# Where the row scale and the first two SwiGLU gates are issued in the opening of each FFN

## The chip, the cores and the metric

The kernel runs on one core of one Trainium2 chip. The time is the device time of one execution of the whole program in microseconds (us); each number for a kernel is the median of several runs. The core has five engines that each work off a queue of their own in order: TensorE (PE in the profile; PEld is its loading of weights), VectorE (DVE), ScalarE (ACT), GpSimd (POOL) and SyncE (SP), which here only issues transfers. They wait for each other through semaphores. SBUF is the on-chip memory; PSUM is the accumulator memory, eight banks of 128 x 512 floats.

## What is computed

A decoder trunk of two layers over 512 tokens of width 1024. Each layer is a half-step SwiGLU FFN, a token mixer (retention in layer 0, forgetting attention in layer 1), a second half-step FFN and a gated per-layer input (PLE). So there are four FFNs, FFN 0 to FFN 3. What matters here is one of them:

```
def rmsnorm(x, w):
    y = x * lax.rsqrt(jnp.mean(x * x, axis=-1, keepdims=True) + EPS)
    return y * w

def swiglu(x, w_in, w_out):
    g, u = jnp.split(x @ w_in, 2, axis=-1)
    return (jax.nn.silu(g) * u) @ w_out

h = h + 0.5 * swiglu(rmsnorm(h, nw[0]), ffn_w_in[i, 0], ffn_w_out[i, 0])
```

The inner width is 2816, which makes 22 pairs of 128 gate rows and 128 up rows.

## The kernel before

Everything is kept transposed, features on the partitions and the 512 tokens along the free axis. Each float32 operand is split into a high and a low part (`split`, line 299: ACT writes the rounded high part, L302; DVE the difference, L303), and a product is made of three matmuls. Weights come through `wraw` tiles (SP's queue, L75), are split by ACT and DVE (L82, L83) or by ACT and an accumulating transfer that GpSimd issues (L120 to L122), and stand in a pool of three tiles, two ahead of use.

The norm's gain is applied to the input, but its scale, one number for each token, is applied after the matmuls. It is made in two steps. `Norm.columns` (line 441) sums the squares on PE (L326) and takes the reciprocal root on ACT and DVE (L464 to L468), which gives `cols`, the scale with tokens on partitions. `Norm.rows` (line 450) transposes `cols` on PE, four matmuls of 128 x 128 into a bank (L459), and ACT copies them to `rows` (L453), in which form the gates use it.

An FFN (`ffn`, line 503) goes through its 22 pairs. The first two are plain (`plain`, line 511): 96 matmuls of 256 columns for one pair (L524), over 16 steps (k, t) of six matmuls. The other 20 pairs use Strassen's form in Winograd's variant with seven products instead of eight, twelve matmuls of 256 columns each (`product`, L493). It is cut into `one` (two products), `two` (one product, and then part of the recombination: ACT copies g to `cc`, L542; DVE adds it to u, L543; ACT copies the sum, L545; DVE adds that to g, L546), `three` (four products into the same banks g and u) and `finish` (the rest of the recombination and the gate). The sums of weights that these products need are made on DVE (L151) and split like the rest (`emit_sums_now`, line 142); in FFN 0 DVE and ACT also make the input's Strassen forms (`quarters`, line 369: L376, L377 and the lines around them) while the plain pairs run.

`gated` (line 564) is the SwiGLU gate of one pair: DVE multiplies g by `rows` (L566), ACT takes the Silu (L567, which loads its table when another function's was in use), DVE multiplies by u (L569 or L571), and `split` makes the two parts (L302, L303) that the output blocks multiply later.

The opening of an FFN stands at lines 592 to 602. In order of issue: the first plain pair, `columns`, the second plain pair, `rows`, `one` of the first Strassen pair (pair 2), the gates of both plain pairs (0 and 1), `two` of pair 2. Then the loop of line 604 issues `one` and `two` of pair 3, `three` and `finish` of pair 2, and so on, one pair ahead; after six, fourteen and all 22 pairs come the output blocks (`out_blocks`).

Only PE's order is written by hand (`manual_schedule`, line 190). The order of ACT, DVE, GpSimd and SP is made when the program is built, by a planner that goes by the order of issue and by its own estimates of when an operand or a buffer is ready; on the chip each queue is then worked off in that order, and an instruction that waits holds what is behind it. Buffers come from pools: eight banks, seven tiles `tmp`.

Of the kernel before, what the change touches and what calls it, by code (L numbers as in the profile page):

```python
# [187 lines left out]
def trunk(ctx, tc, a):  # L188
# [18 lines left out]
    def unit(pool):  # L207
        return pool.tile([P, S], F32R, name="unit_" + {id(ua): "a", id(ub): "b", id(uc): "c", id(ud): "d"}[id(pool)])
# [78 lines left out]
    def bank():  # L287
        return psum.tile([P, S], F32, name="bank")

    def temp(dtype=F32):  # L290
        return tmp.tile([P, S], dtype, name="tmp")
# [7 lines left out]
    def split(src, hi, lo, scale=None):  # L299

        if scale is None:
            high = nc.scalar.copy(hi, src)  # L302
            low = nc.vector.tensor_tensor(out=lo, in0=src, in1=hi.bitcast(F32), op=ALU.subtract)  # L303
        else:
            high = nc.scalar.activation(hi, src, AF.Identity, scale=scale)
            low = nc.vector.scalar_tensor_tensor(
                out=lo, in0=src, scalar=scale, in1=hi.bitcast(F32), op0=ALU.mult, op1=ALU.subtract
            )
        return high, low

    def mm3(out, wh, wl, xh, xl, first, last):
        nc.tensor.matmul(out, wh, xh, start=first, stop=False)  # L312
        nc.tensor.matmul(out, wh, xl, start=False, stop=False)  # L313
        nc.tensor.matmul(out, wl, xh, start=False, stop=last)  # L314
# [175 lines left out]
    def product(out, w, c, forms, name, first=False):  # L490

        xs = [form[name] for form in forms]
        add = lambda w, x, start, stop: nc.tensor.matmul(  # L493
            out, w, x, start=start, stop=stop, skip_group_check=True
        )
        for j, (xh, xl) in enumerate(xs):
            wh = w[:, 0, c + j * P : c + (j + 1) * P]
            add(wh, xh, first and j == 0, False)
            add(wh, xl, False, False)
        for j, (xh, xl) in enumerate(xs):  # L500
            add(w[:, 1, c + j * P : c + (j + 1) * P], xh, False, j == 3)

    def ffn(i, n, nxt, stack, apool, meanwhile=None):


        ins, outs = ffn_src[i]
        chunks = CHUNKS[i]
        c0, c1 = HALVES
        live, act = {}, {}

        def plain(m):

            ws = [W.take(ins[m].q), W.take(ins[m].r)]
            g, u = bank(), bank()
            order = [(k, t) for k in range(KB) for t in range(2)]
            if i:
                order.sort(key=lambda kt: kt[1])
            for k, t in order:
                e = k % 2
                for o, (w, c) in ((g, (ws[e], 0)), (u, (ws[1 - e], 512))):  # L520
                    ks = slice(c + k // 2 * P, c + (k // 2 + 1) * P)
                    xh, xl = n.forms[k // 2][f"b{1 + e}{1 + t}"]
                    for q, (x, y) in enumerate(((w[0], xh), (w[0], xl), (w[1], xh))):
                        nc.tensor.matmul(  # L524
                            o[:, HALVES[t]], x[:, ks], y, start=k == t == q == 0, stop=k == KB - 1 and q == 2,
                            skip_group_check=True,
                        )
            return g, u

        def start(m):  # L530
            live[m] = W.take_pair(ins[m]), bank(), bank()

        def one(m):
            pair, g, u = live[m]
            product(g[:, c0], pair.t, 0, n.forms, "b11", True)
            product(g[:, c1], pair.s[0], 0, n.forms, "t1")

        def two(m):
            pair, g, u = live[m]
            product(u[:, c1], pair.s[1], 0, n.forms, "t2", True)  # L540
            cc = temp()
            nc.scalar.copy(cc, g)  # L542
            nc.vector.tensor_tensor(out=u[:, c1], in0=u[:, c1], in1=cc[:, c0], op=ALU.add)  # L543
            u2 = temp()[:, c0]
            nc.scalar.copy(u2, u[:, c1])  # L545
            nc.vector.tensor_tensor(out=g[:, c1], in0=g[:, c1], in1=u2, op=ALU.add)  # L546
            live[m] += (cc,)

        def three(m):
            pair, g, u, cc = live[m]  # L550
            product(u[:, c0], pair.t, 512, n.forms, "t4")
            product(g[:, c1], pair.s[3], 0, n.forms, "b22")
            product(u[:, c1], pair.s[2], 0, n.forms, "t3")
            product(g[:, c0], pair.x, 0, n.forms, "b21")

        def finish(m):
            pair, g, u, cc = live.pop(m)
            u3 = temp()[:, c0]
            nc.scalar.copy(u3, u[:, c1])
            nc.vector.tensor_tensor(out=u[:, c1], in0=u[:, c1], in1=cc[:, c1], op=ALU.add)  # L560
            nc.vector.tensor_tensor(out=u[:, c0], in0=u[:, c0], in1=u3, op=ALU.add)
            gated(m, g, u, False)

        def gated(m, g, u, change_sign):
            sg = temp()
            nc.vector.tensor_tensor(out=sg, in0=g, in1=n.r, op=ALU.mult)  # L566
            nc.scalar.activation(sg, sg, AF.Silu)  # L567
            if change_sign:
                nc.vector.scalar_tensor_tensor(out=sg, in0=u, scalar=-1.0, in1=sg, op0=ALU.mult, op1=ALU.mult)  # L569
            else:  # L570
                nc.vector.tensor_tensor(out=sg, in0=u, in1=sg, op=ALU.mult)  # L571
            hi, lo = unit(apool), unit(apool)
            split(sg, hi, lo)
            act[m] = hi, lo

        def out_blocks(c, ms):
            k0, k1 = chunks[c]
            os, ws = [bank() for _ in ms], [W.take(outs[c][m]) for m in ms]
            for k in range(k0, k1):
                js = slice((k - k0) * P, (k - k0 + 1) * P)  # L580
                for o, (wh, wl) in zip(os, ws):
                    mm3(o, wh[:, js], wl[:, js], *act[k], k == k0, k == k1 - 1)
            for m, o in zip(ms, os):
                t1 = temp()
                nc.vector.scalar_tensor_tensor(  # L585
                    out=t1, in0=o, scalar=-0.5, in1=n.r, op0=ALU.mult, op1=ALU.mult
                )
                nc.vector.tensor_tensor(out=h[m], in0=h[m], in1=t1, op=ALU.add)
                if c == len(chunks) - 1:
                    nxt.block(m)  # L590

        done = PLAIN[i]
        whole = [plain(m) for m in range(done - 1)]
        W.begin(n.columns())
        whole.append(plain(done - 1))
        n.rows()
        start(done)
        one(done)
        for m, (g, u) in enumerate(whole):
            gated(m, g, u, True)  # L600
        two(done)
        begun = done + 1
        for c, (k0, k1) in enumerate(chunks):
            for m in range(done, k1):
                if begun < k1:
                    start(begun)
                    one(begun)
                    two(begun)
                    begun += 1
                three(m)  # L610
                finish(m)
            done = k1
            if begun < NF:
                start(begun)
                one(begun)
                two(begun)
                begun += 1
            else:
                stack.close()
                if meanwhile:  # L620
                    meanwhile()
            for ms in ((0, 1), (2,), (3,), (4,), (5,), (6,), (7,)):
                out_blocks(c, ms)
# [588 lines left out]
    def ffn_ple(i, l, n, mid, nxt, stack, apool, parts):  # L1212
        phi, plo = [], []

        def load():
            pv = a["pT"][l].rearrange("(b p) t -> b p t", p=P)
            for b in range(2):
                t1 = temp()
                nc.sync.dma_start(out=t1, in_=pv[b])
                phi.append(unit(uc))  # L1220
                plo.append(unit(uc))
                split(t1, phi[b], plo[b])

        ffn(i, n, mid, stack, apool, load)
        stack = open_ffn(i + 1) if i < 3 else None
        ple(l, mid, nxt, phi, plo, parts)
        return stack

    ffn(0, norms[0], norms[1], stack, ud)
    stack = retention(norms[1], norms[2])  # L1230
    stack = ffn_ple(1, 0, norms[2], norms[3], norms[4], stack, ud, 1)
    ffn(2, norms[4], norms[5], stack, ua)
    stack = forgetting(norms[5], norms[6])
    ffn_ple(3, 1, norms[6], norms[7], norms[8], stack, ua, 2)
# [94 lines left out]
```

## Time and profile before

| | |
|---|---|
| median of 3 runs | 2216.24 us (2215.52 to 2218.65) |
| the profiled execution, its own time | 2215.98 us |
| its span, first to last instruction | 2214.2 us |
| mean granted clock of TensorE | 0.990 |
| PE idle in the span | 2214.2 - 2148.7 = 65.5 us |

The profile is one execution. A line of an engine's order of time gives the start from the span's begin, the time to the end of the group, engine, source line, operation, what it writes and reads, and how many instructions were merged; behind them in brackets is the idle time of the engine just before and who ended it. Instructions of one engine overlap a little, so that the distance from start to start is the pace. A line of the waits gives the engine and what it was to do, for whom it waited, and the total, the number and the longest of these waits.

### The profile page before, as it was taken

The page shows a single profiled execution, that of the slowest core. Times are in us where ns is not written, and L with a number is a line of the kernel's source. Part 1 is how long each engine was busy: PE and PEld are TensorE (multiplying, and loading weights), DVE is VectorE, ACT ScalarE, POOL GpSimd, SP SyncE. Part 2 cuts the span into 40 slices and gives each one's busy share as a digit, 9 for nine tenths or more (in the row PEclk, how much of TensorE's full clock was granted, in tenths as well). Part 3 has the DMA queues.
Part 4 walks back from the last instruction along what each step waited for, and adds up shares of the span by engine and source line. Part 5 has one row for each costly group of instructions (what it writes and reads, how often), then busy time and mean ns, then how long its engine had stood idle before and what let it go on. Part 6 is the DMA issues. An engine that isn't in the chain of part 4 may idle for free.

```text
span 2214.2 us, 34442 instructions
## 1 busy us (share of the span) xinstructions
PE 2148.7 (97%) x13525; PEld 1933.3 (87%) x13525; DVE 1459.4 (66%) x2631; ACT 1203.1 (54%) x2027; POOL 466.8 (21%) x352
## 2 busy tenths in 40 slices
PE   7999999999999999999998999999999999999997
PEld 7999997888888798989887989898788898999987
DVE  8687776352533677867758677675575686777764
ACT  7565453343333564746545646364786775554643
POOL 0011013444344000101142001012243200110154
PEclk9999999999999999999999999999999999999999
DMA  5465562222222244645523456373622234655631
GB/s 174 111 168 150 141 163 95 74 94 81 94 78 86 77 126 128 167 126 149 144 92 97 117 142 178 117 166 102 154 86 86 77 112 113 162 155 142 156 105 39
DMA packets 85315, 267.08 MB, mean 121 GB/s; under 512 B 9360, under 2 KB 12944, under 8 KB 85152
## 3 DMA queue, kind: packets, MB, share of 16 engines
q1 hardware_dynamic: 63328, 209.78, 28.0%
q0 software_dynamic: 20592, 54.01, 14.4%
q8 instruction: 106, 1.74, 0.3%
q10 hardware_dynamic: 1232, 1.09, 0.1%
q14 instruction: 57, 0.47, 0.1%
HBM read 262.71 MB, written 2.13 MB: 120 GB/s over the span
## 4 chain that ended last, share of the span: by engine, by line
PE 81%; DVE 7%; ACT 5%; issue 4%; DMA 3%; POOL 1%; SPq 0%; DVEq 0%; ACTq 0%; POOLq 0%
PE bank L493 31%; PE bank L314 13%; PE bank L312 13%; PE bank L313 13%; PE bank L524 3%; DMA wraw<-in_ffn_w_in 2%; PE bank L678 2%; PE bank L679 2%; PE bank L680 2%; DVE w L83 1%; POOL w L83 1%; ACT p L982 1%; ACT w L82 1%; DVE sums L151 1%; DVE tlo L303 1%
## 5 line engine op out<-in xcount | busy, mean ns | idle before, releaser
L82 ACT CAST w<-wraw 128x1024 fp32r<-128x1024 f32 (+1 forms) x242 | 245.5, 1022 | 439.7 <-PE bank L314 257.3
L314 PE MATMUL bank<-unit_a,w 128*128 128x512 f32 x736 | 287.9, 391 | 4.3 <-DVE w L83 2.6
L312 PE MATMUL bank<-unit_a,w 128*128 128x512 f32 x736 | 289.2, 393 | 1.9 <-ACT w L82 1.6
L313 PE MATMUL bank<-unit_a,w 128*128 128x512 f32 x736 | 287.2, 390 | 0.2 <-DVE unit_a L303 0.2
L83 POOL TENSOR_TENSOR w<-wraw,w 128x1024 fp32r<-128x1024 f32 x93 | 226.5, 2439 | 273.7 <-ACT w L82 259.6
L314 PE MATMUL bank<-unit_d,w 128*128 128x512 f32 (+1 forms) x712 | 267.8, 376 | 4.7 <-DVE w L83 4.7
L312 PE MATMUL bank<-unit_d,w 128*128 128x512 f32 (+1 forms) x712 | 268.9, 378 | 3.3 <-ACT w L82 1.6
L82 ACT CAST s<-sums 128x512 fp32r<-128x512 f32 x320 | 191.1, 617 | 146.6 <-DVE sums L151 100.8
L313 PE MATMUL bank<-unit_d,w 128*128 128x512 f32 (+1 forms) x712 | 268.0, 376 | 1.7 <-DVE unit_d L303 1.7
L83 DVE TENSOR_TENSOR s<-sums,s 128x512 fp32r<-128x512 f32 x320 | 213.8, 686 | 83.1 <-ACT s L82 82.0
L122 POOL DMA_DIRECT2D a<-in_ffn_w_in x80 | 70.3, 878 | 654.4 <-ACT a L121 448.0
L83 DVE TENSOR_TENSOR w<-wraw,w 128x1024 fp32r<-128x1024 f32 (+1 forms) x149 | 175.8, 1185 | 23.4 <-ACT w L82 23.3
L493 PE MATMUL bank<-unit_b,s 128*128 128x256 f32 x880 | 185.4, 277 | 0.0
L493 PE MATMUL bank<-unit_d,s 128*128 128x256 f32 x1140 | 178.3, 276 | 0.0
L493 PE MATMUL bank<-unit_a,s 128*128 128x256 f32 x1260 | 176.1, 277 | 1.9 <-ACT unit_a L376 1.1
L585 DVE SCALAR_TENSOR_TENSOR tmp<-bank,rows 128x512 f32<-128x512 f32 x96 | 66.1, 690 | 166.3 <-PE bank L314 165.1
L314 PEld LDWEIGHTS bank<-unit_a,w 128*128 128x128 f32 x736 | 138.5, 188 | 35.7 <-DVE w L83 4.4
L312 PEld LDWEIGHTS bank<-unit_a,w 128*128 128x128 f32 x736 | 138.6, 188 | 32.3 <-ACT w L82 3.5
L313 PEld LDWEIGHTS bank<-unit_a,w 128*128 128x128 f32 x736 | 138.7, 188 | 28.7 <-DVE unit_a L303 0.5
L493 PEld LDWEIGHTS bank<-unit_a,s 128*128 128x128 f32 x1260 | 158.8, 188 | 2.7 <-ACT unit_a L376 1.6
L314 PEld LDWEIGHTS bank<-unit_d,w 128*128 128x128 f32 x712 | 134.1, 188 | 30.8 <-DVE w L83 6.6
L312 PEld LDWEIGHTS bank<-unit_d,w 128*128 128x128 f32 x712 | 134.1, 188 | 30.1 <-ACT w L82 3.3
(268 smaller groups left out, 4780.1 us busy)
## 6 DMA issues: line engine op xcount, KB each, us to landing
wraw<-in_ffn_w_in SPq DMA_DIRECT2D x174, 512.0 KB, 4.3
wraw<-in_ffn_w_out SPq DMA_DIRECT2D x64, 512.0 KB, 4.7
w<-in_ffn_w_in POOLq DMA_DIRECT2D x56, 512.0 KB, 5.3
a<-in_ffn_w_in POOLq DMA_DIRECT2D x80, 256.0 KB, 6.2
wraw<-in_ffn_w_out SPq DMA_DIRECT2D x32, 384.0 KB, 3.5
wraw<-in_ret_qk SPq DMA_DIRECT2D x16, 512.0 KB, 3.5
wraw<-in_ret_v SPq DMA_DIRECT2D x16, 512.0 KB, 3.6
wraw<-in_ret_g SPq DMA_DIRECT2D x16, 512.0 KB, 3.4
```

The source lines that it names most:

```text
L82: self.nc.scalar.copy(hi, raw)
L83: self.low.tensor_tensor(out=lo, in0=raw, in1=hi.bitcast(F32), op=ALU.subtract)
L122: self.nc.gpsimd.dma_start(out=lo, in_=src, accum_op=ALU.add)
L312: nc.tensor.matmul(out, wh, xh, start=first, stop=False)
L313: nc.tensor.matmul(out, wh, xl, start=False, stop=False)
L314: nc.tensor.matmul(out, wl, xh, start=False, stop=last)
L493: add = lambda w, x, start, stop: nc.tensor.matmul(out, w, x, start=start, stop=stop, skip_group_check=True)
L524: nc.tensor.matmul(o[:, HALVES[t]], x[:, ks], y, start=k == t == q == 0, stop=k == KB - 1 and q == 2, skip_group_check=True,)
L585: nc.vector.scalar_tensor_tensor(out=t1, in0=o, scalar=-0.5, in1=n.r, op0=ALU.mult, op1=ALU.mult)
L678: nc.tensor.matmul(os[t], xh, wh[:, js], start=k == 0, stop=False)
L679: nc.tensor.matmul(os[t], xh, wl[:, js], start=False, stop=False)
L680: nc.tensor.matmul(os[t], xl, wh[:, js], start=False, stop=k == KB - 1)
```

## The change

`plain` gets an optional function `between`, which is called before the eleventh of the 16 steps, that is after 60 of the 96 matmuls. For the second plain pair this function issues `rows` and the gate of the first plain pair. So PE makes the four transposes inside that pair. The gate of the second plain pair is issued behind `two` of pair 2, that is behind its L542 to L546. No instruction is added or dropped.

```
-        def plain(m):
+        def plain(m, between=None):
...
-            for k, t in order:
+            for at, (k, t) in enumerate(order):
+                if at == 10 and between:
+                    between()
...
         whole = [plain(m) for m in range(done - 1)]
         W.begin(n.columns())
-        whole.append(plain(done - 1))
-        n.rows()
+
+        def scaled():
+            n.rows()
+            for m, (g, u) in enumerate(whole):
+                gated(m, g, u, True)
+
+        last = plain(done - 1, scaled)
         start(done)
         one(done)
-        for m, (g, u) in enumerate(whole):
-            gated(m, g, u, True)
         two(done)
+        gated(done - 1, *last, True)
         begun = done + 1
```

## The prediction, made before the changed kernel was run

> **What bounds the kernel now.** I read the page first, then PE's waits, then the order of time of each engine around the openings of the four FFNs, where the changed lines run, and last the granted clock in stretches picked from there.
>
> ```profile
> span 2214.2 us, 34442 instructions
> PE 2148.7 (97%) x13525; PEld 1933.3 (87%) x13525; DVE 1459.4 (66%) x2631; ACT 1203.1 (54%) x2027; POOL 466.8 (21%) x352
> ```
>
> TensorE (PE) is the bound: it idles for 2214.2 - 2148.7 = 65.5 us. The change adds and drops no instruction, so all it can win is idle time, and the time in which PE runs at a lower clock. PE's waits, longest first in total (us, times, longest):
>
> ```profile
> PE bank L493 <- ACT tmp L545: 14.2, 6, 5.5
> ```
>
> This is the largest wait of PE, and four of its six cases lie in the openings, one in each FFN (start, duration; in brackets the idle time before):
>
> ```profile
> 55.83 2.93 PE L493 MATMUL bank<-unit_a,w 128*128 128x256 f32 x12 [5.54 <-ACT tmp L545]
> 814.10 0.50 PE L493 MATMUL bank<-unit_b,w 128*128 128x256 f32 x2 [2.28 <-ACT tmp L545]
> 1231.70 0.50 PE L493 MATMUL bank<-unit_b,w 128*128 128x256 f32 x2 [2.28 <-ACT tmp L545]
> 1830.25 0.51 PE L493 MATMUL bank<-unit_b,w 128*128 128x256 f32 x2 [2.40 <-ACT tmp L545]
> ```
>
> Each time PE has reached three(2), whose first product goes into the bank that L543 adds into and L545 reads: the recombination of pair 2, issued in two(2), comes too late. The stalls are 5.54 + 2.28 + 2.28 + 2.40 = 12.50 us. What follows them is slower too. The next table holds the 24 matmuls behind each stall, and in its second row the same 24 a pair later in FFN 0 (PEclk is the granted clock):
>
> ```profile
> core 0: us, PE busy (x) PEld busy (x) DVE busy (x) ACT busy (x) POOL busy (x), PEclk, DMA share, GB/s
> 55.83:60.87 5.04, 5.04 (x25) 5.04 (x26) 2.96 (x6) 3.79 (x6) 0.00 (x0) 0.53 0.11 43
> 67.84:70.64 2.80, 2.80 (x26) 2.80 (x25) 2.25 (x5) 2.00 (x4) 0.00 (x0) 1.00 0.97 252
> 814.10:818.56 4.46, 4.46 (x25) 4.46 (x25) 2.16 (x5) 3.33 (x5) 0.00 (x0) 0.62 0.01 6
> 1231.70:1234.59 2.89, 2.89 (x25) 2.89 (x25) 2.16 (x5) 2.49 (x5) 0.00 (x0) 1.00 0.06 21
> 1830.25:1833.15 2.90, 2.90 (x25) 2.90 (x25) 2.16 (x5) 2.49 (x5) 0.00 (x0) 1.00 0.02 10
> ```
>
> Against 2.80 us, the 24 took 2.24, 1.66, 0.09 and 0.10 us longer, 4.09 in all; in the first two the clock stood at 0.53 and 0.62. So stalls and their wake are worth at most 12.50 + 4.09 = 16.6 us.
>
> **Why the recombination is late.** ACT, then DVE, in FFN 1:
>
> ```profile
> 802.80 1.05 ACT L82 CAST w<-wraw 128x1024 fp32r<-128x1024 f32 x1 [6.19 <-PE bank L524]
> 806.26 1.28 ACT L567 ACT_TABLE_LOAD   x1
> 810.18 0.56 ACT L542 COPY tmp<-bank 128x512 f32<-128x512 f32 x1
> 813.15 0.62 ACT L302 CAST unit_d<-tmp 128x512 fp32r<-128x512 f32 x1 [1.89 <-DVE tmp L569]
> 813.68 0.37 ACT L545 COPY tmp<-bank 128x256 f32<-128x256 f32 x1
> ...
> 808.22 0.69 DVE L569 SCALAR_TENSOR_TENSOR tmp<-bank,tmp 128x512 f32<-128x512 f32 x1 [1.91 <-ACT tmp L567]
> 811.23 0.68 DVE L303 TENSOR_TENSOR unit_d<-tmp,unit_d 128x512 fp32r<-128x512 f32 x1
> 812.44 0.68 DVE L569 SCALAR_TENSOR_TENSOR tmp<-bank,tmp 128x512 f32<-128x512 f32 x1
> 813.04 0.42 DVE L543 TENSOR_TENSOR bank<-bank,tmp 128x256 f32<-128x256 f32 x1
> ...
> 807.50 0.64 PE L493 MATMUL bank<-unit_b,w 128*128 128x256 f32 x4
> 811.43 0.39 PE L493 MATMUL bank<-unit_a,s 128*128 128x256 f32 x2
> ```
>
> PE has done two(2) at 807.50, and one(3) and two(3) cover it until about 811.7. In these 4.2 us L542, L543, L545 could run: steps of 0.56, 0.42 and 0.37 us. But each engine works off its queue in order, and ahead of them stand both gates: the scale's copy, a table load of 1.28 us, two Silus and a cast on ACT, two L569 and an L303 on DVE, with 1.91 us in which DVE waits for the Silu. All that bunches behind the second plain pair, for which ACT idled 6.19 us just before.
>
> **The change, FFN 1 to 3.** Moved: four transposes on PE, the copy L453 on ACT, and gate 0 (three steps of DVE, two of ACT and the table load); none issues a DMA, and the queues of SP and POOL are passed by nothing. Gate 0 goes into ACT's hole. The transposes come before the 61st of the pair's 96 matmuls; they cost PE what they cost at their old place. The 36 matmuls behind them, and all after, now wait for the scale, cols, at this point:
>
> ```profile
> 34.10 0.28 PE L524 MATMUL bank<-unit_b,w 128*128 128x256 f32 x1
> 31.33 0.15 DVE L468 SCALAR_TENSOR_TENSOR cols<-ct,cols 128x4 f32<-128x4 f32 x1
> 798.59 0.88 PE L524 MATMUL bank<-unit_d,w 128*128 128x256 f32 x6
> 795.20 0.15 DVE L468 SCALAR_TENSOR_TENSOR cols<-ct,cols 128x4 f32<-128x4 f32 x1
> ```
>
> Cols is there at 31.48 in FFN 0 and 795.35 in FFN 1; PE comes to the 61st matmul at 34.10 and 798.59. With 2.6 and 3.2 us to spare I take nothing for this wait. If DVE's order changed, it would cost whatever goes beyond that (a rival below).
>
> From 798.6 gate 0 then takes, in a row, about 0.4 (transposes, an estimate: four matmuls at the pace of the 96), 0.6 for the copy, estimated from L542, 0.7, 1.28, 0.6, 0.7, 0.6 and 0.7 us: done near 804, where ACT and DVE otherwise begin on the next weights. Its last cast may hold the L82 of 802.80 by some 0.6 us; that weight is wanted at 807.50 and has its cast by 803.9, so I book zero. In ACT's queue ahead of L542 some 3.4 us are gone (copy 0.5, load 1.28, two Silus and a cast at 0.53 each), so L542 starts as soon as its product is there. On DVE three steps of 0.60 and the 1.91 us of waiting are gone ahead of L543: 813.04 - 3.7 = 809.3, and L545 ends 1.0 later, at 810.3. PE wants it at 811.7. The stall goes whole in FFN 1, and as FFN 2 and 3 show stalls of the same size behind the same L545, there too: (2.28 + 1.66) + (2.28 + 0.09) + (2.40 + 0.10) = 8.81 us. Gate 1 moves behind L546 and is needed by the output blocks only, pairs later; it falls into this hole of DVE:
>
> ```profile
> 819.41 0.69 DVE L83 TENSOR_TENSOR s<-sums,s 128x512 fp32r<-128x512 f32 x1 [3.15 <-ACT s L82]
> ```
>
> Its three DVE steps need 1.8 of 3.15 us, so nothing is late next.
>
> **The change, FFN 0.** Here ACT and DVE also make the other forms of the input, and DVE has no pause from 39.64 on:
>
> ```profile
> 39.64 1.21 DVE L377 TENSOR_TENSOR unit_a<-tmp,unit_a 128x256 fp32r<-128x256 f32 x2 [3.14 <-ACT unit_a L376]
> 44.21 0.68 DVE L566 TENSOR_TENSOR tmp<-bank,rows 128x512 f32<-128x512 f32 x1
> 49.96 0.68 DVE L569 SCALAR_TENSOR_TENSOR tmp<-bank,tmp 128x512 f32<-128x512 f32 x1
> 53.57 0.68 DVE L303 TENSOR_TENSOR unit_d<-tmp,unit_d 128x512 fp32r<-128x512 f32 x1
> 54.17 0.68 DVE L566 TENSOR_TENSOR tmp<-bank,rows 128x512 f32<-128x512 f32 x1
> 54.77 0.42 DVE L543 TENSOR_TENSOR bank<-bank,tmp 128x256 f32<-128x256 f32 x1
> ```
>
> Ahead of L543 the three steps of gate 0 and the first of gate 1 go, at 0.60 each (54.17 to 54.77): 2.4 us, the first three into the hole of 3.14. The rest of DVE's queue, sums of weights, stays. So L545 comes 2.4 earlier and 3.1 of the 5.54 us stay. Bounds: zero, if gate 0 is planned behind the forms, to 5.54, if L543 also passes the sums of later pairs. For the wake I take half of 2.24, since of the three stalls of 2.28 to 2.40 us one drew a low clock and two did not: 1.1, with 0 and 2.24 as ends. FFN 0 gives 3.5.
>
> [...]
>
> **Sum.** 8.81 + 3.5 = 12.3 us, off the profiled execution's 2215.98 (span 2214.2 and 1.8 around it): 2203.7. The median of the runs, 2216.24, lies 0.26 above; I say 2204.
>
> **Rivals.** *All goes:* FFN 0 keeps nothing either; 16.6 us, 2199.6. For it: 36 matmuls of cover there too. Against: DVE is full from 39.64 to 54.77.
> *The first gate does not really move:* the other engines' orders are a planner's, by its own estimates; it may put gate 0 behind the next weights and forms all the same. Then only gate 1 leaves the queue: one DVE step (0.60) and one Silu (0.53) per FFN, four times 1.1: 4.5 us, 2211.7. Against it: ACT's idle 6.19 us, with nothing else ready.
> *Slower: the scale is late.* PE stands at the transposes, in mid-pair, with nothing else to do. Should each of the four links of the chain to cols fall behind two casts' differences of 1.2 us, it ends 9.6 us later; less the 2.6 and, taking FFN 2 and 3 like FFN 1, three times 3.2 to spare, PE loses 7.0 + 3 x 6.4 = 26 us against 12.3 won: 2230. It decides from a delay of about 6 us on. Against: nothing ahead of L468 in issue order is moved.
>
> **How the numbers follow.** Forecast 0.60, all goes 0.15, first gate stays 0.20, late scale 0.05. About 0.2%, 4.4 us, can be told from no change. The first two are faster by more, and of the third, which sits on that edge, a third: 0.60 + 0.15 + 0.06 = 0.81; the rest of it, 0.14, is within 0.2%; slower 0.05. The range goes from the full gain, 2199, to 2212, just past the third case's price; beyond it lie the late scale and some of the third case.
>
> **What would show it.** Right: no idle before three(2) in FFN 1 to 3 and some 3 us in FFN 0; L453 and the Silu's table load ahead of the L82 that waits for the second plain pair; L542 to L546 ahead of the second L566; clock 1.00 behind. Wrong: PE idle at L459, or L545 again last behind a cast, Silu or L569.

## The result and the profile after

The changed kernel takes 2197.6 us (median of 4 runs, 2196.54 to 2200.27) against 2215.88 us of the kernel before beside it (4 runs). The ratio is 0.9922, its 95% interval 0.9905 to 0.9938, which is 13.7 to 21.1 us. I had said 2204, within 2199 to 2212: the direction was right, the size was not, and the median lies 1.4 us under the range.

The page of the changed kernel (its own time 2196.75 us, mean clock 0.994); then PE's waits for the first Strassen pair's recombination. The source lines behind line 511 have moved: L524 is now L526, L542 to L546 are L544 to L548, L566, L567 and L569 are L568, L569 and L571.

```profile
span 2195.0 us, 34450 instructions
PE 2140.7 (98%) x13525; PEld 1927.3 (88%) x13525; DVE 1455.9 (66%) x2631; ACT 1201.0 (55%) x2027; POOL 466.3 (21%) x352
```
```profile
PE bank L493 <- ACT tmp L547: 3.1, 2, 1.7
PE bank L493 <- DVE bank L548: 0.7, 1, 0.7
```

The span is 19.2 us shorter. PE idles 54.3 us instead of 65.5, and it is busy 8.0 us less, with the same 13525 matmuls: the second part is clock (0.994 against 0.990 in the mean), not waiting. Each engine's count is the same; the 8 instructions more in the page's total are not among them. The wait that led the list, 14.2 us in six cases, is 3.1 in two.

FFN 2 shows what I had expected of FFN 1 to 3 (ACT, then DVE, then PE):

```profile
1201.53 0.59 ACT L453 COPY rows<-bank 128x512 f32<-128x512 f32 x1 [2.84 <-PE bank L459]
1202.13 1.28 ACT L569 ACT_TABLE_LOAD   x1
1205.52 1.05 ACT L82 CAST w<-wraw 128x1024 fp32r<-128x1024 f32 x1 [1.09 <-PE bank L526]
1209.41 0.58 ACT L544 COPY tmp<-bank 128x512 f32<-128x512 f32 x1
1210.61 0.37 ACT L547 COPY tmp<-bank 128x256 f32<-128x256 f32 x1
...
1210.15 0.42 DVE L545 TENSOR_TENSOR bank<-bank,tmp 128x256 f32<-128x256 f32 x1
1212.62 0.68 DVE L568 TENSOR_TENSOR tmp<-bank,rows 128x512 f32<-128x512 f32 x1
...
1209.80 0.64 PE L493 MATMUL bank<-unit_b,w 128*128 128x256 f32 x4
1213.96 0.40 PE L493 MATMUL bank<-unit_b,w 128*128 128x256 f32 x2
```

The scale's copy and the table load stand ahead of the L82 that waits for the second plain pair. The recombination follows the end of two(2), 1209.80, and is through on ACT at 1210.98; PE comes to three(2) at 1213.96 and does not wait. Gate 1's first step runs behind it, at 1212.62.

FFN 0 came out otherwise (ACT, DVE, PE):

```profile
37.04 1.05 ACT L82 CAST w<-wraw 128x1024 fp32r<-128x1024 f32 x1 [0.94 <-PE bank L526]
45.49 1.28 ACT L569 ACT_TABLE_LOAD   x1
48.35 0.61 ACT L302 CAST unit_d<-tmp 128x512 fp32r<-128x512 f32 x1
48.88 0.36 ACT L547 COPY tmp<-bank 128x256 f32<-128x256 f32 x1
...
44.86 0.68 DVE L568 TENSOR_TENSOR tmp<-bank,rows 128x512 f32<-128x512 f32 x1
46.66 0.42 DVE L545 TENSOR_TENSOR bank<-bank,tmp 128x256 f32<-128x256 f32 x1
51.20 0.42 DVE L548 TENSOR_TENSOR bank<-bank,tmp 128x256 f32<-128x256 f32 x1
...
49.29 1.69 PE L493 MATMUL bank<-unit_a,w 128*128 128x256 f32 x12 [1.69 <-ACT tmp L547]
51.68 0.86 PE L493 MATMUL bank<-unit_b,s 128*128 128x256 f32 x5 [0.70 <-DVE bank L548]
```

Gate 0 did not go into the pause: its product stands at 44.86, against 44.21 before. Forms of the input went there instead (ACT's idle time ahead of the L82 is 0.94 us, it was 3.64). Yet DVE's L545 comes at 46.66, 8.1 us earlier than its forerunner at 54.77 (in a1, a control below whose second plain pair ran faster, the forerunner stood at 53.40: 6.7 us). What is left, 1.69 + 0.70 us, is no longer DVE's queue alone: the sum was there at 47.1, and ACT's copy of it stood behind the table load, the Silu, two casts of sums and the gate's cast until 48.88.

### The profile page after: what moved, and what is told of

Read it like the earlier page. It is cut to its first block, busy times and chain, and to the rows that moved or that the text cites. A ratio compares the mean times of both kernels' runs of the same rounds, so it can differ in the third digit from the quotient of the medians.

```text
span 2195.0 us, 34450 instructions
## 1 busy us (share of the span) xinstructions
PE 2140.7 (98%) x13525; PEld 1927.3 (88%) x13525; DVE 1455.9 (66%) x2631; ACT 1201.0 (55%) x2027; POOL 466.3 (21%) x352
## 4 chain that ended last, share of the span: by engine, by line
PE 83%; DVE 6%; ACT 4%; issue 4%; DMA 2%; POOL 1%; SPq 0%; DVEq 0%; ACTq 0%; POOLq 0%
PE bank L493 33%; PE bank L314 13%; PE bank L312 13%; PE bank L313 13%; PE bank L526 3%; PE bank L685 2%; PE bank L684 2%; PE bank L686 2%; DMA wraw<-in_ffn_w_in 1%; DVE w L83 1%; POOL w L83 1%; ACT p L988 1%; ACT w L82 1%; ACT p L990 1%; DVE tlo L303 1%
## 5 line engine op out<-in xcount | busy, mean ns | idle before, releaser
L82 ACT CAST w<-wraw 128x1024 fp32r<-128x1024 f32 (+1 forms) x242 | 245.6, 1022 | 421.2 <-PE bank L314 255.3
L82 ACT CAST s<-sums 128x512 fp32r<-128x512 f32 x320 | 191.6, 617 | 153.9 <-DVE sums L151 101.9
```

Source lines behind the costliest of these rows:

```text
L82: self.nc.scalar.copy(hi, raw)
```

## The experiments

The theory after this look, called the queue theory below: PE's stall before three(2) is the recombination's place in the queues of ACT and DVE; what the change wins is this idle time, and also the lower clock that such idle time draws behind it (0.53 in FFN 0 and 0.62 in FFN 1 over the 24 matmuls), which I had priced from one execution. Rivals: only one of the moves counts; or the clock's part is luck that has nothing to do with the stalls (the clock theory). Twelve kernels ran; a time is given as the ratio to the kernel before on the same chip, in us of 2216.

**The two controls.** a1 is the kernel before and a2 the changed one, neither edited.

> The kernel before, unchanged, as a control against itself. Queue theory (the gain is the stalls before three(2) and what they do to the clock behind them): ratio 1.000 within 0.002, and the same four stalls of 5.5, 2.3, 2.3 and 2.4 us. Clock theory (part of the gain is the place of stretches of 3.41 us of half clock that no changed line decides): the stretches near 381, 747 and 815 us of the first profile stand elsewhere or are missing here, and the span differs by up to 1.7 us for each, though the queues are the same.

Ratio 1.0002 (0.9987 to 1.0017). The stalls are the same to 0.01 us: 5.54, 2.27, 2.27 and 2.40. But the 24 matmuls behind those of FFN 1, 2 and 3, timed as in the prediction, are not:

```profile
811.58:816.05 4.47, 4.47 (x25) 4.47 (x26) 2.16 (x5) 3.24 (x5) 0.00 (x0) 0.62 0.03 13
1227.29:1231.60 4.31, 4.31 (x24) 4.31 (x25) 2.16 (x5) 3.33 (x5) 0.00 (x0) 0.64 0.04 14
1826.92:1829.82 2.90, 2.90 (x25) 2.90 (x25) 2.17 (x5) 2.50 (x5) 0.00 (x0) 1.00 0.04 14
```

FFN 2's stall drew the low clock here, 0.64, and in the first profile it had not (2.89 us at clock 1.00).

> The changed kernel, unchanged. Queue theory: 15 to 16 us faster than before, 2200 to 2201: 11.2 us less idle time of TensorE and some 4 us of half clock behind the stalls. Clock theory: the 19.2 us between the first two profiles hold some 3 us of luck, so this profile comes out with other stretches of half clock and the gain between 13 and 20.

Ratio 0.9918 (0.9895 to 0.9941), 18.2 us. The openings of FFN 1 to 3 last the same to 0.01 us as in the first profile of the changed kernel, and FFN 0 keeps 1.71 and 0.70 us of stall. The span was 2200.5, 5.5 us more than the first time. Of these, 3.6 lie near 1465 us, where PE waited 2.0 us that it had not waited before, and the other 1.6 I put down to the clock behind that wait; 2.8 come in the first 30 us; and 1.5 are saved near 2124 us, where the clock of the first profile stood at 0.51 (2123.80 to 2127.30). The scatter between executions of one kernel is, as I read it, of this kind.

**The stages apart.** The new opening in FFN 0 alone (a3), and in the other three alone (a4):

```
+        if i == 0:        # a4: if i > 0
+            last = plain(done - 1, scaled)
...
+        else:
+            whole.append(plain(done - 1))
+            n.rows()
...
```

> The change in FFN 0 alone, the other three FFNs with their queues as before. Queue theory by the first two profiles: 6.2 us faster (5.0 at the stall of 5.54 and its wake, 1.2 inside one(2)), stalls of FFN 1 to 3 unchanged at 2.3, 2.3 and 2.4 us. My forecast's term was 3.5. Clock theory: 3 to 8, as the stretches fall.

> The change in FFN 1, 2 and 3 alone, FFN 0 with its queues as before. Queue theory: the three stalls of 2.3 to 2.4 us go whole, 7.0 us, and up to 1.9 us of their wake: 7.0 to 8.9 faster (my forecast's term was 8.8). FFN 0 keeps 5.5 us. With the FFN 0 part the two gains add up to the whole one within 2 us. Clock theory: 5 to 11.

FFN 0 alone: 0.9967 (0.9952 to 0.9981), 7.3 us, between 4.2 and 10.6. The other three: 0.9948 (0.9928 to 0.9968), 11.5 us, between 7.1 and 16.0. The two make 18.8, the whole change 18.2: they add up. My terms were 3.5 and 8.8. The three stalls that a3 keeps drew the low clock all three, 0.62 to 0.69:

```profile
810.77:815.23 4.46, 4.46 (x24) 4.46 (x25) 2.16 (x5) 3.33 (x5) 0.00 (x0) 0.62 0.04 17
1226.39:1230.48 4.09, 4.09 (x25) 4.09 (x26) 2.16 (x5) 3.33 (x5) 0.00 (x0) 0.69 0.03 13
1829.06:1833.35 4.29, 4.29 (x24) 4.29 (x25) 2.16 (x5) 2.65 (x5) 0.00 (x0) 0.65 0.01 6
```

So of nine stalls of 2.3 to 2.4 us in three profiles (the first, a1, a3) six drew it, at 1.6 to 1.8 us each over the 48 matmuls of three(2), and three did not, at 0.1: 1.2 us in the mean.

**The moves apart.** b1 puts gate 1 back ahead of two(2); b2 keeps the scale and gate 0 at their old place; b3 moves the scale alone into the pair and both gates behind two(2); c1 moves the scale alone and leaves both gates at their old place.

```
b1:      one(done)
+        gated(done - 1, *last, True)
         two(done)
-        gated(done - 1, *last, True)

b2 (on the kernel before):
-        for m, (g, u) in enumerate(whole):
-            gated(m, g, u, True)
+        gated(0, *whole[0], True)
         two(done)
+        gated(1, *whole[1], True)

b3 and c1, in scaled():
             n.rows()
-            for m, (g, u) in enumerate(whole):
-                gated(m, g, u, True)
```

> Half of the change: scale and gate 0 inside the second plain pair, but gate 1 at its old place ahead of two(2). Queue theory, by the orders of the queues: in FFN 1 to 3 five vector steps more stand ahead of L543 than in the changed kernel, 3.0 us, which brings L545 to where PE wants it, so stalls of 0 to 0.6 us there and some 6 to 8 us won; in FFN 0 gate 1's product and both multiplications by u come back ahead of L543, the stall stays at 5 to 6 us. Together 6 to 9 us faster than before. Rival (only the early scale and gate count): 15 us, like the whole change.

Ratio 0.9954 (0.9938 to 0.9969), 10.2 us. No stall in FFN 1 to 3, and in FFN 0 the old one:

```profile
55.07 2.93 PE L493 MATMUL bank<-unit_a,w 128*128 128x256 f32 x12 [5.49 <-ACT tmp L547]
```

> The other half: scale and gate 0 at their old place, gate 1 behind two(2). Queue theory: two vector steps and a Silu leave the queue ahead of L543 and L545, 1.2 us in each FFN, stalls of about 1.0 in FFN 1 to 3 and 4.5 in FFN 0: 5 us faster than before, up to 9 with the wake. Rival (the order of gate 1 alone is what counts): 15 us, like the whole change.

Ratio 0.9985 (0.9971 to 0.9999), 3.3 us, between 0.2 and 6.4. The stalls are shorter by 0.8 to 0.9 us each, where I had expected 1.2:

```profile
53.54 2.93 PE L493 MATMUL bank<-unit_a,w 128*128 128x256 f32 x12 [4.65 <-ACT tmp L545]
811.36 0.51 PE L493 MATMUL bank<-unit_b,w 128*128 128x256 f32 x2 [1.50 <-ACT tmp L545]
1226.83 0.50 PE L493 MATMUL bank<-unit_b,w 128*128 128x256 f32 x2 [1.49 <-ACT tmp L545]
1823.03 0.50 PE L493 MATMUL bank<-unit_b,w 128*128 128x256 f32 x2 [1.63 <-ACT tmp L545]
```

> The scale inside the second plain pair, but both gates behind two(2): no gate stands ahead of the recombination. Queue theory: no stall in FFN 1 to 3, as in the changed kernel, and in FFN 0 a stall of 1 to 2 us; within 2 us of the changed kernel, 15 us faster than before. Rival (gate 0 has to be done early, for its banks and buffers): pair 4 waits for gate 0's banks, and 3 us or more of the gain are lost.

Ratio 0.9940 (0.9918 to 0.9962), 13.3 us. No stall in FFN 1 to 3, 2.37 us in FFN 0; from the 37th matmul of the second plain pair to the end of three(2) FFN 0 takes 26.0 us, the changed kernel 26.45. Pair 4 does not wait for banks, so that rival falls.

> The scale alone moved into the second plain pair; both gates issued at their old place. Queue theory, by the orders of the queues: in FFN 1 to 3 the planner by itself takes gate 0 up behind the scale, as in the run with gate 0 moved (b1), so no stall there, some 10 us won; in FFN 0 the forms of the input come earlier as in all runs with an early scale, but both products and both multiplications by u stand around L543, so a stall of 4 to 5 us stays there. Together 9 to 11 us faster than before. Rival (the gates' place in the order of issue is what moves them): 2 us faster at most.

Ratio 0.9936 (0.9919 to 0.9953), 14.2 us, more than I had expected. No stall in FFN 1 to 3 beyond 0.2 us, and 3.75 us in FFN 0:

```profile
53.41 2.04 PE L493 MATMUL bank<-unit_a,w 128*128 128x256 f32 x12 [3.75 <-ACT tmp L547]
```

So in FFN 1 to 3 moving the scale alone is enough. How the gates get out of the way differs. In c1 the planner takes gate 0 into ACT's pause by itself (FFN 1, ACT):

```profile
793.73 1.28 ACT L569 ACT_TABLE_LOAD   x1
797.12 1.05 ACT L82 CAST w<-wraw 128x1024 fp32r<-128x1024 f32 x1 [1.46 <-issue]
```

In b3 the pause stays empty and both gates follow the recombination:

```profile
795.07 1.05 ACT L82 CAST w<-wraw 128x1024 fp32r<-128x1024 f32 x1 [3.40 <-PE bank L526]
800.63 0.38 ACT L547 COPY tmp<-bank 128x256 f32<-128x256 f32 x1 [0.47 <-DVE bank L545]
803.04 1.28 ACT L569 ACT_TABLE_LOAD   x1
```

No run left the scale at its old place and put both gates behind two(2), so it is not shown that FFN 1 to 3 need the early scale at all. Gate 1's place counts in FFN 0, where 5.49 us stay without it and 2.4 with it. Gate 0's own place in the order of issue does nothing that these runs can tell (b3 against the changed kernel).

**The scale too early.** b4 calls scale and gate 0 after 24 matmuls:

```
-                if at == 10 and between:
+                if at == 4 and between:
```

> The changed kernel with the scale and gate 0 called after 24 of the pair's 96 matmuls in place of 60. Late-scale rival at work: PE comes to the transposes 36 matmuls, 4.3 us, earlier, where cols had 2.6 to 4.9 us to spare; so PE idles at L459 for 0 to 1.7 us in FFN 0 and FFN 1 to 2, and nothing in FFN 3 (estimates from the margins), 2 to 4 us in all lost against the changed kernel. If PE does not wait for cols at all, the time is the changed kernel's within 1 us.

Ratio 0.9929 (0.9902 to 0.9956), 15.7 us. The late scale is real, PE's wait at the transposes:

```profile
PE bank L459 <- DVE cols L468: 4.4, 3, 2.9
```

2.9 us in FFN 0, where I had expected at most 1.7, and 0.8 and 0.7 in FFN 1 and 2. What it costs in FFN 0 it gives back there: no stall before three(2) is left. The medians, 2200.6 here and 2199.7 for the changed kernel in its own rounds, cannot be told apart.

**The clock by itself.** The kernel before with its stalls filled. c2 put the filling matmuls behind two(3):

```
+                if m == PLAIN[i]:
+                    for _ in range(44 if i == 0 else 18):
+                        nc.tensor.matmul(live[m + 1][1][:, c0], zero_r, n.forms[0]["b11"][0], start=False, stop=False, skip_group_check=True)
                 three(m)
```

> The kernel before, with its four stalls filled: ahead of three(2) TensorE makes 44 (FFN 0) and 18 (FFN 1 to 3) matmuls of a zero weight into a bank that nobody reads yet; they add zeros. Nothing else comes earlier. Queue theory with a price for the clock: three(2) starts where it started, but the clock stays at full behind it, so the wakes alone go: by the three profiles with stalls 1.2 us each in FFN 1 to 3 and some 2 in FFN 0, 5 to 6 us faster than before. If the wake is no more than the first profile showed, 4.1 us. Rival (the wake is not the idle's doing): no change.

It failed as an experiment: 1.0100 (1.0083 to 1.0117), 22 us slower, because I had put the matmuls behind the L548 that adds to the same bank, and they waited for it:

```profile
PE bank L614 <- DVE bank L548: 22.7, 4, 9.1
```

d1 issues the same matmuls inside two(3), right behind its product.

> The filled stall once more, mended: in the last run the filling matmuls themselves waited for L548 of pair 3 and stood 22.7 us, so it told nothing of the clock. Now they come inside two(3), right behind its product, ahead of all that reads the bank. The kernel is the one before otherwise; TensorE makes 44 (FFN 0) and 18 (FFN 1 to 3) matmuls of a zero weight, 5.0 and 2.1 us, while it would stand before three(2). Queue theory with a price for the clock: three(2) starts as before, within 0.3 us, and its first 24 matmuls take 2.8 to 2.9 us in all four FFNs, with the granted clock at full; 4 to 6 us faster than before. Rival (low clock behind a stall comes from something else than TensorE's idle time): they take 4.3 us and more in some of them, and no change in time.

Ratio 0.9963 (0.9946 to 0.9979), 8.2 us faster, between 4.7 and 12.0, with PE doing 98 matmuls more and nothing else coming earlier: three(2) begins as long after one(2) as in the kernel before, to 0.01 us in each FFN. The 24 matmuls behind each filled stall:

```profile
55.59:58.49 2.90, 2.90 (x25) 2.90 (x26) 2.54 (x5) 2.64 (x5) 0.00 (x0) 1.00 0.25 97
809.97:812.87 2.90, 2.90 (x25) 2.90 (x26) 1.82 (x4) 2.27 (x4) 0.00 (x0) 1.00 0.01 6
1223.44:1226.34 2.90, 2.90 (x25) 2.90 (x25) 1.83 (x4) 2.27 (x4) 0.00 (x0) 1.00 0.04 14
1823.55:1826.44 2.89, 2.89 (x25) 2.89 (x25) 1.83 (x4) 2.27 (x4) 0.00 (x0) 1.00 0.03 11
```

Full clock, 1.00, behind all four, where six of the nine stalls left unfilled had 0.62 to 0.69. The low clock behind the stalls is the idle time's doing, and it alone costs the kernel before 4.7 us or more by this run's interval.

**What was left in FFN 0.** c3 is the changed kernel with the steps of two(2) put ahead of the others in the planner's order:

```
+        with tc.high_priority():
             two(done)
```

> The changed kernel, with the steps of two(2) ahead of all others in the planner's order. Queue theory: what is left of the stall in FFN 0, 1.7 us at L547 behind a Silu, its table load, two casts of sums and a cast of the gate, and 0.7 at L548 behind two sums, falls to 0 to 0.5 us, as U2 now stands right behind the Silu; 2 us faster than the changed kernel, 17 to 20 faster than before. FFN 1 to 3 unchanged without a stall. Rival (DVE is full there, so anything put ahead makes the forms or the sums of pair 3 late instead): a new wait of the same size in one(3), two(3) or three(2).

Ratio 0.9912 (0.9896 to 0.9929), 19.5 us faster than before. L547 now stands right behind the Silu, and PE waits 0.1 us for it (ACT, then PE):

```profile
48.09 0.64 ACT L569 ACTIVATE tmp<-tmp 128x512 f32<-128x512 f32 x1
48.62 0.35 ACT L547 COPY tmp<-bank 128x256 f32<-128x256 f32 x1
48.88 1.14 ACT L82 CAST s<-sums 128x512 fp32r<-128x512 f32 x2
...
49.03 1.70 PE L493 MATMUL bank<-unit_a,w 128*128 128x256 f32 x12
```

From the 37th matmul of the second plain pair to the end of three(2), FFN 0 takes 23.8 us, 2.7 less than in the changed kernel, and nothing else there waits more. The median, 2196.6 against 2197.6 and 2199.7, is the lowest of all, but 2.7 us is less than the intervals can tell from the changed kernel.

## Why the prediction missed, point by point

- *The four stalls are the recombination behind the gates in the queues of ACT and DVE.* Right. The halves of the change shorten the stalls where the queues say so, and where at most gate 0's cast and difference are left between the second plain pair and L545 there is none (FFN 1 to 3 in a2, a4 and b3). In b1 gate 1 still stands there as well, and in FFN 1 L547 ends at 808.10, just ahead of three(2) at 808.16.
- *FFN 1 to 3 lose their stall whole, L545 at 810.3 against 811.7.* Right; FFN 2 had 3.0 us to spare.
- *Their wake is 1.66 + 0.09 + 0.10.* Wrong size, and the first term that failed. "Wake" was read from one execution, in which two of three stalls happened to draw nothing. Over three profiles it is 1.2 us a stall, so 3.6 in place of 1.85. With it, an opening of FFN 1 to 3 lasts 31.30 us in the mean of nine (the first profile, a1, a3), from the sums on PE to the end of three(2), and 27.63 in the changed kernel: 3 x 3.67 = 11.0 us, against 8.8 said and 11.5 measured.
- *In FFN 0, "the rest of DVE's queue, sums of weights, stays", so 3.1 of 5.54 us stay.* The step that failed in working. Gate 0 did not go into the pause, so the reason for the 2.4 us was wrong. The early scale let the planner take the forms into it, which shortens one(2) and two(2) from 7.2 to 6.1 us; and with gate 1 issued later, L545 passed three sums of pair 4: nine L151 stand ahead of it in place of twelve, and with gate 1 back in its place (b1) there are twelve again. From the 37th matmul of the second plain pair to the end of three(2), FFN 0 takes 32.1 us in the mean of three profiles with the old opening (the first, a1, a4) and 26.45 in all three with the new one (the first, a2, a3): 5.7 us against 3.5 said.
- *The ceiling, 16.6 us, was the range's lower end.* It was no ceiling: it held the same one-execution wake, and no term for one(2). The sum with the sizes above is 5.7 + 11.0 = 16.7 us, inside both measured intervals (13.7 to 21.1 and 13.1 to 23.3). The medians lie 1.5 us further; of that nothing is shown, and a chance stretch of low clock elsewhere would be enough for it: an estimate, from the 3.41 us at 0.50 that begin at 381.39 in the first profile of the kernel before, which make 1.7 us.
- *The first gate does not really move.* True in FFN 0, and it did no harm. In FFN 1 to 3 it went as forecast.
- *The late scale.* Not met at 60 matmuls. It is there at 24, so the mechanism was right. The margin of 3.2 us was of the right size (3.4 in FFN 1 of the changed kernel). The 2.6 of FFN 0 held for that execution: in the changed kernel's first profile cols is there at 31.02 and PE at the transposes at 32.46, 1.4 us, which is also what b4's wait of 2.9 leaves of the 4.3 us by which it comes earlier.
- *What follows the stalls is slower too.* Right, but not in each execution. The measured stalls of 2.3 to 2.4 us drew the low clock in six of nine cases, 0.62 to 0.69 over the 24 matmuls behind them, and filling them took it away (d1, 1.00 behind all four).

## What to carry to other kernels

A stall on the bounding engine costs more than its length where its clock falls behind it (1.6 to 1.8 us more behind six stalls of nine here): price both, and take the second from several profiles, since in one execution a stall may draw the low clock or miss it (last section). Before moving work, look whether the planner already moves it: here the operand that came late (the scale) was the thing to issue early, and most of the gain followed from that alone (14.2 us in c1, 18.2 for the whole change). And where a queue is full, a step that leaves it lets the planner order everything behind it anew, so that "the rest stays" is an assumption with a price of its own.

## What the runs showed of the hardware that I had not expected

The same stall drew the low clock or not from execution to execution: FFN 2's in the opening had 0.64 behind it in a1 and 1.00 in the first profile. One outside the changed lines shows it in both kernels, a wait for GpSimd in the retention. Before, the wait and the 3.4 us behind it:

```profile
380.55 0.50 PE L314 MATMUL bank<-unit_a,w 128*128 128x512 f32 x1 [1.71 <-POOL w L83]
...
381.40:384.80 3.40, 3.40 (x10) 2.63 (x9) 2.94 (x3) 0.64 (x2) 1.88 (x1) 0.50 0.61 188
```

After, the same wait and what follows it:

```profile
372.78 0.51 PE L314 MATMUL bank<-unit_a,w 128*128 128x512 f32 x1 [1.70 <-POOL w L83]
...
372.78:376.20 3.42, 3.42 (x15) 2.84 (x16) 3.34 (x4) 0.62 (x1) 2.76 (x1) 1.00 0.48 153
```

Behind 1.71 us of idle time the clock stood at 0.50, from 0.84 us after its end on; behind 1.70 us it stayed at 1.00. In the trace's records of the granted clock, the first profile of the kernel before has seven stretches at 0.50. The three shortest, from 381.39, 746.61 and 814.88 us, last 3.41 us each with PE busy throughout.

What decides whether a stall draws such a stretch was not shown. The stalls of FFN 1 and 2, 2.3 us, drew it in five of six cases and those of FFN 3, 2.4 us, in one of three, and no run here made gaps of a chosen length or place.
